# Where the operands of 17,280 matmuls stand in SBUF: high and low parts side by side, moving operands 0 or 256 bytes (modulo 512) from the weights loaded beside them

## The chip, the cores and the metric

The kernel runs on one core of one Trainium2 chip. The metric is the device time of one execution in microseconds, the median of several runs. All weights come from HBM in every execution; nothing of them stays on the chip between executions.

## What is computed

One inference step of a two-layer trunk with model width 2048 for a prompt of 256 new tokens and 8 samples of 4 tokens each, which share the weights. Layer 0 mixes by retention and a gated linear recurrence, layer 1 by a diagonal state-space model (S5) and a GLU; both end in a SwiGLU feed-forward (FFN) with 5632 hidden channels.

```python
# per layer (rmsnorm, silu and gelu as usual)
out, *states = even_mixer(x, ...)   # layer 0: w_in 2048x6144, retention | conv + RG-LRU, w_out 2048x2048
out, *states = odd_mixer(x, ...)    # layer 1: S5 scan, gelu, w_glu 2048x4096, z1 * sigmoid(z2)
x = x + out
x = x + swiglu(rmsnorm(x, g))       # w_gu 2048x11264, w_dn 5632x2048
y = rmsnorm(x, g_final)
# returned: y of the prompt and of the samples, and the new states
```

256 + 32 tokens make 288 columns, N in the code.

## The kernel before

**The products.** Channels lie on partitions and tokens along the free dimension, so every dense product is a row of matmuls of one shape: a stationary 128 x 128 block of weights, a moving operand of 128 x 288. float32 inputs go through the fast float32r path by splitting each operand into a high part (what float32r keeps) and a low part (the rest), and by summing three products in PSUM for each block k of the contraction, in this order (lines 315 to 317 in `run_prog`):

```python
pe.matmul(acc, lhsT=wh[:, o:o + P], rhs=xh, start=(k == u.k0), stop=False)
pe.matmul(acc, lhsT=wh[:, o:o + P], rhs=xl, start=False, stop=False)
pe.matmul(acc, lhsT=wl[:, o:o + P], rhs=xh, start=False, stop=(k == u.k1 - 1))
```

I call these three a triple. While one matmul streams its moving operand, TensorE loads the weights of the next one from SBUF. So the high part of a chunk streams beside the load of the same block of `wh` (for the second matmul), the low part beside the load of a block of `wl`, and the high part once more beside the load of the next block of `wh`.

**The weights.** `run_prog` walks through all units (one unit is 128 output channels) in slots of up to 8 blocks. For each slot SP loads `raw` by DMA (ring of 4), ScalarE writes the high part `wh` (ring of 4, line 268), VectorE the low part `wl` (line 274, which appears as line 99; 3 buffers, from the first FFN on a fourth, `wlx`). All of them are tiles of 128 x 1024 float32, 4096 bytes in each partition. A block is 512 bytes long, so within one ring all blocks start at the same place modulo 512. In the built program that is byte 32 for `raw`, `wh` and the three `wl`, and byte 288 for `wlx`.

**The moving operands.** A chunk is 128 x 288 float32, 1152 bytes in each partition, which is 2 x 512 + 128. Chunks come out of pools (helpers `xg_`, `xl_`, `ac_`, called through `split`), which hand out a ring of buffers that lie one after the other:
- `xg_`, `xl_`: 16 high parts and behind them 16 low parts of the normed input (w_in, FFN 0, and the high parts of FFN 1). From one chunk to the next both move by 128 bytes modulo 512.
- `ac_`: one ring in which high and low parts alternate (20 buffers in the first phase, 30 later), for the input of w_out, the hidden channels of both FFNs and the high parts of the GLU's input. High and low part of one chunk are 128 bytes apart modulo 512, and the next chunk of a unit stands wherever the ring had come to.
- `x2`: the low parts of FFN 1's input, in a pool that is opened after the S5 stage (line 1583).

With weights at byte 32 (or 288) a moving operand stands at 0, 128, 256 or 384 bytes from the weights loaded beside it, and in the program before these four are taken by 4504, 4095, 4250 and 4113 of the matmuls that another of these follows (some 240 have other distances, in w_out).

**Other buffers.** `g_` hands out scratch tiles of a ring: 11 in the first phase, 14 later (`phase_open`). The order of the instructions is that of the Python code: `later` puts a step some slots further on, and each engine runs its queue in order.

**The S5 stage** (`s5_core`) has small matmuls of 72 columns between which VectorE works. Matmuls without use, `warm` (line 1475), keep TensorE going there: 24 ahead of the stage and 8, 8, 8 and 16 in its first four steps, all with weights at column 512 of a `wh` tile and a moving operand from column 0 on, so 0 bytes apart modulo 512; they have 64 or 128 columns of weights and 128, 288 or 512 moving columns.

## Time and profile before

| | |
|---|---|
| median of 3 runs | 2492.91 us (2488.81 to 2494.98) |
| the profiled execution | 2491.51 us, of which the span is 2489.7 us |
| TensorE busy | 2449.2 us, 98% of the span |
| VectorE, ScalarE, GpSimd busy | 66%, 46%, 6% |
| DMA | 198 GB/s on average |
| granted TensorE clock, mean | 0.996 |

The program runs w_in and w_out to about 460 us, FFN 0 to about 1340 us, S5 with the first part of the GLU to about 1480 us, the rest of the GLU to about 1630 us, and FFN 1 to the end. A matmul's duration in a row (about 295 ns) is its latency from first read to last write; matmuls overlap, so what counts is the distance from one start to the next, which is read from timelines, or from the number of matmuls in a window.

### The profile page before, as it was taken

To read this page: it belongs to the slowest core of one execution; us is meant where nothing else is said; L and a number is where in the kernel's file an instruction comes from. 1 tells how busy PE (TensorE), PEld (TensorE's weight loads), DVE (VectorE), ACT (ScalarE), POOL (GpSimd) and SP (SyncE) were. 2 spreads that over 40 slices of the span, in tenths; PEclk is the share of its full clock that TensorE was granted. 3 is DMA by queue.
4 is the path that set the end of the run, shared out by engine and by line. 5 is a ranking of instruction groups with operands and counts; after the bars stand their busy time and mean duration, and the time that the engine had idled before them with its cause. 6 is when DMAs were issued, how large, how long until landed. Compare 5 with 4: busy or idle time off the path is not lost.

```text
span 2489.7 us, 49585 instructions
## 1 busy us (share of the span) xinstructions
PE 2449.2 (98%) x20130; PEld 2419.2 (97%) x20130; DVE 1638.0 (66%) x3033; ACT 1145.3 (46%) x1756; POOL 154.2 (6%) x299
## 2 busy tenths in 40 slices
PE   8999999999999999999999999999999999999997
PEld 8999999999999999999998899999999999999997
DVE  7767676567677878778856996655544555445554
ACT  6656554533355445555543554443333333333343
POOL 0111110000010121111110000000000000000000
PEclk9999999999999999999999999999999999999999
DMA  7655655555577777777797875555555555555553
GB/s 250 192 183 187 214 163 172 168 163 165 185 243 250 254 257 249 257 262 227 241 294 223 291 235 159 184 164 162 165 163 171 162 167 157 169 167 163 162 164 127
DMA packets 168612, 493.78 MB, mean 198 GB/s; under 512 B 30400, under 2 KB 42944, under 8 KB 168128
## 3 DMA queue, kind: packets, MB, share of 16 engines
q1 hardware_dynamic: 152192, 439.51, 55.7%
q0 software_dynamic: 15184, 49.77, 5.7%
q8 instruction: 159, 2.61, 0.4%
q10 hardware_dynamic: 1008, 1.33, 0.1%
q14 instruction: 69, 0.57, 0.1%
HBM read 449.16 MB, written 48.19 MB: 200 GB/s over the span
## 4 chain that ended last, share of the span: by engine, by line
PE 92%; DVE 4%; DMA 2%; ACT 1%; issue 1%; SPq 0%; DVEq 0%; ACTq 0%
PE acc L315 30%; PE acc L317 29%; PE acc L316 29%; DVE w L99 1%; DVE wl L99 1%; DMA tab<-tabO 1%; DMA raw<-in_w_glu_dram 1%; DMA raw<-in_w_in_dram 1%; DMA tab<-tabR 0%; DVE w L1459 0%; PE mp L775 0%; PE mp L520 0%; PE mp L1310 0%; ACT wh L268 0%; PE mp L723 0%
## 5 line engine op out<-in xcount | busy, mean ns | idle before, releaser
L315 PE MATMUL acc<-xg,wh 128*128 128x288 f32 x3520 | 1045.6, 297 | 0.0
L268 ACT ACTIVATE wh<-raw 128x1024 fp32r<-128x1024 f32 (+2 forms) x758 | 760.4, 1010 | 427.6 <-PE acc L316 262.7
L317 PE MATMUL acc<-xg,wl 128*128 128x288 f32 x2816 | 828.1, 294 | 1.3 <-DVE wl L99 1.3
L316 PE MATMUL acc<-xl,wh 128*128 128x288 f32 x2624 | 773.8, 295 | 0.0
L99 DVE TENSOR_TENSOR wl<-raw,wh 128x1024 fp32r<-128x1024 f32 (+3 forms) x601 | 697.5, 1173 | 24.6 <-ACT wh L268 16.3
L315 PEld LDWEIGHTS acc<-xg,wh 128*128 128x128 f32 x3520 | 659.6, 187 | 1.8 <-issue 0.8
L315 PE MATMUL acc<-ac,wh 128*128 128x288 f32 x2080 | 616.7, 297 | 2.0 <-ACT ac L1594 1.1
L317 PEld LDWEIGHTS acc<-xg,wl 128*128 128x128 f32 x2816 | 530.4, 188 | 1.5 <-DVE wl L99 1.5
L316 PEld LDWEIGHTS acc<-xl,wh 128*128 128x128 f32 x2624 | 493.0, 188 | 0.5
L317 PE MATMUL acc<-ac,wl 128*128 128x288 f32 x1626 | 480.8, 296 | 3.4 <-DVE wl L99 2.4
L316 PE MATMUL acc<-ac,wh 128*128 128x288 f32 x1568 | 462.6, 295 | 0.0
L316 PE MATMUL acc<-x,wh 128*128 128x288 f32 x1408 | 415.4, 295 | 0.0
L315 PEld LDWEIGHTS acc<-ac,wh 128*128 128x128 f32 x2080 | 391.6, 188 | 4.8 <-ACT ac L1594 1.3
L99 DVE TENSOR_TENSOR g<-acc,rstd 128x288 f32<-128x288 f32 x192 | 87.7, 457 | 347.5 <-PE acc L317 346.9
L317 PEld LDWEIGHTS acc<-ac,wl 128*128 128x128 f32 x1626 | 306.5, 189 | 5.9 <-DVE wl L99 5.9
L316 PEld LDWEIGHTS acc<-ac,wh 128*128 128x128 f32 x1568 | 296.1, 189 | 0.0
L316 PEld LDWEIGHTS acc<-x,wh 128*128 128x128 f32 x1408 | 264.3, 188 | 0.1
L317 PE MATMUL acc<-xg,wlx 128*128 128x288 f32 x704 | 207.0, 294 | 0.0
L99 DVE TENSOR_TENSOR X<-X,acc 128x288 f32<-128x288 f32 x112 | 50.9, 455 | 233.7 <-PE acc L317 233.4
L99 DVE TENSOR_TENSOR wlx<-raw,wh 128x1024 fp32r<-128x1024 f32 (+3 forms) x157 | 178.6, 1138 | 17.9 <-ACT wh L268 17.7
L194 ACT ACTIVATE ac<-g 128x288 fp32r<-128x288 f32 x98 | 43.5, 444 | 283.8 <-DVE g L99 283.8
L317 PE MATMUL acc<-ac,wlx 128*128 128x288 f32 x454 | 133.7, 295 | 0.1
(294 smaller groups left out, 2038.2 us busy)
## 6 DMA issues: line engine op xcount, KB each, us to landing
raw<-in_w_gu_dram SPq DMA_DIRECT2D x352, 512.0 KB, 4.6
raw<-in_w_dn_dram SPq DMA_DIRECT2D x128, 448.0 KB, 4.2
raw<-in_w_in_dram SPq DMA_DIRECT2D x96, 512.0 KB, 4.7
raw<-in_w_dn_dram SPq DMA_DIRECT2D x64, 512.0 KB, 3.7
raw<-in_w_out_dram SPq DMA_DIRECT2D x32, 512.0 KB, 4.3
raw<-in_w_glu_dram SPq DMA_DIRECT2D x40, 384.0 KB, 4.2
raw<-in_w_glu_dram SPq DMA_DIRECT2D x32, 320.0 KB, 4.0
out_ret_s_dram<-s POOLq DMA_DIRECT2D x16, 512.0 KB, 5.2
```

Of the source, the lines that this page charges most:

```text
L99: v.tensor_tensor(o, a, b, op=op)
L194: act.activation(h, x, AF.Copy, scale=scale)
L268: act.activation(wh[:, :w], raws[i][:, :w], AF.Copy)
L315: pe.matmul(acc, lhsT=wh[:, o:o + P], rhs=xh, start=(k == u.k0), stop=False)
L316: pe.matmul(acc, lhsT=wh[:, o:o + P], rhs=xl, start=False, stop=False)
L317: pe.matmul(acc, lhsT=wl[:, o:o + P], rhs=xh, start=False, stop=(k == u.k1 - 1))
```

## The change

No product, no weight and no order of work is changed, apart from the `warm` matmuls. What changes is where tiles lie:
- `xgp` and the `act` pool have one buffer for each name instead of a ring, and `next_` takes the names in turn. Since a name's place is given at its first use, and `split` now takes the low part before the high part, the tiles of a pair lie side by side: low, high, low, high. A pair is 2304 bytes, which is 4 x 512 + 256, so from pair to pair every high part moves by 256 bytes modulo 512, and so does every low part.
- `ac_` gets a sister, `al_`, for low parts: 10 + 10 names instead of 20 buffers, later 15 + 15 instead of 30.
- a pad of 128 bytes, `wpad`, stands between `raw` and `wh` (byte 32) and the `wl` tiles, which so come to byte 160, `wlx` included. In the built program all high parts in these pools are at byte 32 or 288 and all low parts at 160 or 416.
- the input of FFN 1 is cut from two large tiles at a step of 1536 bytes, high parts in one, low parts in the other.
- the scratch ring has 10 buffers instead of 11, later 13 instead of 14.
- the `warm` matmuls all get 128 columns of weights and 288 moving columns: 32 ahead of the S5 stage, of which 8 are 0, 8 are 256, 8 are 128 and 8 again 256 bytes apart, and 8 in each of the first four steps, at 0, 128, 256 and 384 bytes. (Weights from column 512 on, moving operand from column b on.)

In the built program 10,450 of the 17,280 matmuls are then 256 bytes from the weights loaded beside them and 6432 are 0 bytes from them; some 320 have other distances, in w_out.

```diff
-    xgp = ctx.enter_context(tc.tile_pool(name="xgp", bufs=16))
+    xgp = ctx.enter_context(tc.tile_pool(name="xgp", bufs=1))
...
+    def next_(k, n):
+        turn[k] = turn.get(k, -1) + 1
+        return turn[k] % n
+
     def xg_(dt=F32R):
-        return xgp.tile([P, N], dt, tag="x", name=nm("xg"))
+        return xgp.tile([P, N], dt, tag=f"x{next_('x', 16)}", name=nm("xg"))
...
-    def ac_(dt=F32R, w=N):
-        return AP_["p"].tile([P, AP_["w"]], dt, tag="a", name=nm("ac"))[:, :w]
+    def ac_(dt=F32R):
+        return AP_["p"].tile([P, N], dt, tag=f"a{next_('a', AP_['n'])}", name=nm("ac"))
+
+    def al_(dt=F32R):
+        return AP_["p"].tile([P, N], dt, tag=f"al{next_('al', AP_['n'])}", name=nm("al"))
...
     def split(x, scale, alloc, alloc_l=None, lag=True):
+        l = (alloc_l or alloc)()
         h = alloc()
         act.activation(h, x, AF.Copy, scale=scale)
-        l = (alloc_l or alloc)()
...
+        for tag in ("raw", "wh"):
+            wt.tile([P, 1024], F32R if tag == "wh" else F32, tag=tag, name=nm(tag))
+        wt.tile([P, 32], F32, name="wpad", bufs=1)
         ring = [wt.tile([P, 1024], F32R, name=f"wl{k}", bufs=1) for k in range(3)]
...
-    ph = phase_open(11, 20, N, 6)
+    ph = phase_open(10, 10, 6)
...
-        return split(x, 0.5, ac_)
+        return split(x, 0.5, ac_, al_)
...
-                    hid[t] = split(u, 0.5, ac_)
+                    hid[t] = split(u, 0.5, ac_, al_)
...
-        phase_open(14, 30, N, 0)
+        phase_open(13, 15, 0)
...
-        def warm(ps, n, m, w=N):
+        def warm(ps, n, b):
             xw = S["whs"][min(S["whs"])]
             for k in range(n):
-                o = 32 * (k % 4) if m == 32 else 0
-                pe.matmul(ps[o:o + m, :w], lhsT=xw[:, 512:512 + m], rhs=xw[:, :w], start=True, stop=True,
-                          tile_position=(0, o), skip_group_check=True)
+                pe.matmul(ps[k % len(ps)][:, :N], lhsT=xw[:, 512:640], rhs=xw[:, b:b + N], start=True, stop=True,
+                          skip_group_check=True)
...
-                warm(po, *((8, P), (8, 64), (8, 64), (16, P, P))[j])
+                warm([po], 8, 32 * j)
...
-            h, l = ac_(), xl_()
+            h, l = (ac_ if j < NT - 1 else al_)(), xl_()
...
-        pw = ps5.tile([P, 512], F32, tag="o", name=nm("po"))
-        warm(pw, 10, P, 512)
-        warm(pw, 8, 64)
-        warm(pw, 2, P, 512)
-        warm(pw, 4, P, 512)
+        pw = ps5.tile([P, 2, 512], F32, tag="p", name=nm("pp"))
+        for b in (0, 64, 32):
+            warm([pw[:, 0]], 8, b)
+        warm([pw[:, 0], pw[:, 1]], 8, 64)
...
-        S["x2"] = S["st2"].enter_context(tc.tile_pool(name="x2", bufs=16))
+        S["x2"] = S["st2"].enter_context(tc.tile_pool(name="x2", bufs=1))
...
-        fin = final_hook(V_FFN1, {}, "xg", lambda: S["x2"].tile([P, N], F32R, tag="x", name=nm("x2")))
+        def x2(k):
+            if ("y", k) not in turn:
+                turn["y", k] = S["x2"].tile([P, 384 * NT + 96], F32R, tag=f"y{k}", name=f"x2{k}")
+            i = 384 * next_(k, NT) + 64
+            return turn["y", k][:, i:i + N]
+        fin = final_hook(V_FFN1, {}, "xg", lambda: x2(0), lambda: x2(1))
```

On every engine the instructions stand in the same order before and after, under other tile names, with one exception on TensorE ahead of and in the S5 stage. There the queue of TensorE reads before (`po` and `pp` are PSUM tiles, `tab` a table of the S5 stage, `xg` its input, `Hs` its states; lines 1435, 1489 and 1499 are the small matmuls):

```order
L1416 MATMUL po_16591<-nacc_15595,ones 32x72 x4
L1479 MATMUL po_16611<-wh_16469 128x512 x10
L1479 MATMUL po_16611<-wh_16469 64x288 x8
L1479 MATMUL po_16611<-wh_16469 128x512 x6
L1435 MATMUL pp_16637<-xg_15683,tab_15850 64x72 x16
L1435 MATMUL pp_16657<-xg_15746,tab_15856 64x72 x16
L1479 MATMUL po_16683<-wh_16469 128x288 x8
L1489 MATMUL po_16683<-xg_15683,tab_15854 32x72 x16
```

And in the changed kernel, at the same place:

```order
L1429 MATMUL po_16594<-nacc_15598,ones 32x72 x4
L1491 MATMUL pp_16614<-wh_16472 128x288 x32
L1448 MATMUL pp_16648<-xg_15686,tab_15853 64x72 x16
L1448 MATMUL pp_16668<-xg_15749,tab_15859 64x72 x16
L1491 MATMUL po_16694<-wh_16472 128x288 x8
L1501 MATMUL po_16694<-xg_15686,tab_15857 32x72 x16
```

The 24 `warm` matmuls of two shapes have become 32 of one shape, in the PSUM tile that the stage's first real matmuls use next; nothing else has moved.

Waits on released buffers differ in a few places, since pools are laid out otherwise. The one that changes engine is on ScalarE in the GLU, at the first high part of FFN 1's input. Before (`wh` from `raw` are weights, `xg` is the high part, `nacc` the sum of squares; DMASW are GpSimd's DMA queues, through which the S5 states leave):

```order
L268 ACTIVATE wh2807_19043<-raw2799_18972 128x768 [waits DMAHW2_49,PE_49,Activation_49]
L268 ACTIVATE wh2810_19064<-raw2802_18994 128x640 [waits DMAHW3_49,PE_49,Activation_49]
L194 ACTIVATE xg2814_19087<-X_76,vec_74 128x288 [waits DVE_49]
L173 ACTIVATE nacc2813_19086<-X_76 128x288
L268 ACTIVATE wh2816_19091<-raw2805_19018 128x640 [waits DMAHW4_49,PE_49,Activation_49]
```

And after:

```order
L281 ACTIVATE wh2809_19046<-raw2801_18975 128x768 [waits DMAHW2_49,PE_49,Activation_49]
L281 ACTIVATE wh2812_19067<-raw2804_18997 128x640 [waits DMAHW3_49,PE_49,Activation_49]
L205 ACTIVATE x20_19091<-X_76,vec_74 128x288 [waits DMASW3_49,DMASW4_49,DVE_49,Pool_49]
L183 ACTIVATE nacc2815_19089<-X_76 128x288
L281 ACTIVATE wh2816_19094<-raw2807_19021 128x640 [waits DMAHW4_49,PE_49,Activation_49]
```

The wait for the end of the S5 tables' space, which VectorE had ahead of the first low part, is ScalarE's now, ahead of the first high part.

## Rows read from the trace of the kernel before

**Rows 1.** The page, part 1: busy time, share of the span, instructions of each engine.
```profile
PE 2449.2 (98%) x20130; PEld 2419.2 (97%) x20130; DVE 1638.0 (66%) x3033; ACT 1145.3 (46%) x1756; POOL 154.2 (6%) x299
```

**Rows 2.** Waits of TensorE: line, who was waited for, us in total, times, longest.
```profile
PE mp L315 <- ACT xg L355: 7.4, 1, 7.4
PE po L1499 <- ACT ac L1522: 4.2, 3, 2.5
PE acc L317 <- DVE wl L99: 3.7, 5, 1.3
```

**Rows 3.** Groups of line 315 on TensorE: count, busy us, mean ns, idle before.
```profile
L315 PE MATMUL acc<-xg,wh 128*128 128x288 f32 x3520 | 1045.6, 297 | 0.0
L315 PE MATMUL acc<-ac,wh 128*128 128x288 f32 x2080 | 616.7, 297 | 2.0 <-ACT ac L1594 1.1 <-ACT wh L268 1.0
L315 PE MATMUL acc<-l,wh 128*128 128x288 f32 x96 | 28.3, 295 | 0.0
L315 PE MATMUL mp<-xg,wh 128*128 128x288 f32 x64 | 21.0, 327 | 7.4 <-ACT xg L355 7.4
```

**Rows 4.** Windows of TensorE: us, busy us (matmuls), granted clock, DMA share, GB/s.
```profile
1700.00:1800.00 100.00, 100.00 (x753) 1.00 0.53 168
1800.00:2400.00 600.00, 600.00 (x4506) 1.00 0.51 164
```

**Rows 5.** Timeline of TensorE in FFN 1: start us, duration us, instruction.
```profile
1700.78 0.29 PE L315 MATMUL acc<-xg,wh 128*128 128x288 f32 x1
...
1701.18 0.30 PE L315 MATMUL acc<-xg,wh 128*128 128x288 f32 x1
...
1701.58 0.29 PE L315 MATMUL acc<-xg,wh 128*128 128x288 f32 x1
```

**Rows 6.** Timeline of TensorE in the GLU, first and last of eleven starts.
```profile
1489.56 0.29 PE L316 MATMUL acc<-xl,wh 128*128 128x288 f32 x1
...
1490.86 0.29 PE L317 MATMUL acc<-ac,wlx 128*128 128x288 f32 x1
```

**Rows 7.** Timeline of TensorE in the GLU, six starts in a row.
```profile
1492.81 0.29 PE L317 MATMUL acc<-ac,wl 128*128 128x288 f32 x1
1492.94 0.29 PE L315 MATMUL acc<-ac,wh 128*128 128x288 f32 x1
1493.07 0.30 PE L316 MATMUL acc<-xl,wh 128*128 128x288 f32 x1
1493.21 0.29 PE L317 MATMUL acc<-ac,wl 128*128 128x288 f32 x1
1493.34 0.29 PE L315 MATMUL acc<-ac,wh 128*128 128x288 f32 x1
1493.47 0.29 PE L316 MATMUL acc<-xl,wh 128*128 128x288 f32 x1
```

**Rows 8.** Timeline of TensorE in FFN 1's second product, first and last of 25 starts.
```profile
2136.58 0.29 PE L315 MATMUL acc<-ac,wh 128*128 128x288 f32 x1
...
2139.82 0.29 PE L315 MATMUL acc<-ac,wh 128*128 128x288 f32 x1
```

**Rows 9.** Warm matmuls of S5's steps 0 and 2: timeline, then durations min/median/max ns.
```profile
1354.12 1.32 PE L1479 MATMUL po<-wh 128*128 128x288 f32 x8
1367.88 1.26 PE L1479 MATMUL po<-wh 128*64 128x288 f32 x8
L1479 PE MATMUL po<-wh x8: 290/294/401, 1354.1 to 1355.1; 128*128 128x288 f32 x8
L1479 PE MATMUL po<-wh x8: 288/293/346, 1367.9 to 1368.8; 128*64 128x288 f32 x8
```

**Rows 10.** Warm matmuls of S5's step 1: timeline of TensorE.
```profile
1363.07 2.08 PE L1479 MATMUL po<-wh 128*64 128x288 f32 x8
```

**Rows 11.** The chain of waits ahead of S5: start us, us, what.
```profile
1347.12 4.91 PE po L1479 x24
1353.24 1.30 DVE w L99 x2
```

**Rows 12.** Window at the start of S5: us, busy of PE, PEld, DVE, ACT, POOL, clock.
```profile
1356.00:1364.00 8.00, 5.20 (x107) 4.78 (x101) 7.61 (x13) 2.00 (x6) 0.36 (x1) 0.63 0.65 225
```

**Rows 13.** FFN 1's low parts on VectorE: durations, first and last start.
```profile
L108 DVE SCALAR_TENSOR_TENSOR x<-X,vec,xg x16: 510/514/516, 1494.2 to 1634.5; 128x288 fp32r<-128x288 f32 x16
```

More of the change, by code (lines that the diff above doesn't have):

```diff
@@ L69, in gp_ @@
         return AP_["gen"].tile([P, TOK], dt, tag="g", name=nm("g"))[:, :w]
+    turn = {}
+    def next_(k, n):
+        turn[k] = turn.get(k, -1) + 1
+        return turn[k] % n
     def xg_(dt=F32R):
-        return xgp.tile([P, N], dt, tag="x", name=nm("xg"))
+        return xgp.tile([P, N], dt, tag=f"x{next_('x', 16)}", name=nm("xg"))
     def xl_():
-        return xgp.tile([P, N], F32R, tag="xl", name=nm("xl"))
-    def ac_(dt=F32R, w=N):
-        return AP_["p"].tile([P, AP_["w"]], dt, tag="a", name=nm("ac"))[:, :w]
+        return xgp.tile([P, N], F32R, tag=f"xl{next_('xl', 16)}", name=nm("xl"))
+    def ac_(dt=F32R):
+        return AP_["p"].tile([P, N], dt, tag=f"a{next_('a', AP_['n'])}", name=nm("ac"))
+    def al_(dt=F32R):
+        return AP_["p"].tile([P, N], dt, tag=f"al{next_('al', AP_['n'])}", name=nm("al"))
     AP_ = {}
@@ L83, in mp_, with phase_open @@
         return AP_["ps"].tile([P, 512], F32, tag="m", name=nm("mp"))
-    def phase_open(gb, ab, aw, pb):
+    def phase_open(gb, ab, pb):
         st = AP_["st"] = ExitStack()
         AP_["gen"] = st.enter_context(tc.tile_pool(name=nm("gen"), bufs=gb))
-        AP_["p"] = st.enter_context(tc.tile_pool(name=nm("act"), bufs=ab))
-        AP_["w"] = aw
+        AP_["p"] = st.enter_context(tc.tile_pool(name=nm("act"), bufs=1))
+        AP_["n"] = ab
+        turn["a"] = turn["al"] = -1
         if pb:
@@ L851, in yl_evac, with final_hook @@
         return evac
-    def final_hook(gcol, accbox, lstname, alloc_l=xl_):
+    def final_hook(gcol, accbox, lstname, alloc=xg_, alloc_l=xl_):
         def fin(j):
@@ L859, in fin @@
             if gcol is not None:
-                xs[lstname].append(split(x, vec[:, gcol + j:gcol + j + 1], xg_, alloc_l))
+                xs[lstname].append(split(x, vec[:, gcol + j:gcol + j + 1], alloc, alloc_l))
             norm_acc(accbox["acc"], j, x)
@@ L1596, in first @@
             return Unit(w, 0, k1, lambda: xs["y"], ev)
-        g1 = [first(("g", j), ins["w_glu"][NT + j], 4 if j < 12 else 6, lambda: ac_(F32)) for j in range(NT - 2)]
+        g1 = [first(("g", j), ins["w_glu"][NT + j], 4 if j < 12 else 6, lambda: al_(F32)) for j in range(NT - 2)]
         g1 += [first(("z", j), ins["w_glu"][j], 6, lambda: xg_(F32)) for j in range(NT - 2)]
```

## The prediction, made before the changed kernel ran

> **What bounds the kernel now.** I read the busy times first. TensorE is busy for 2449.2 of 2489.7 us, VectorE for 66% [rows 1]. That alone could be a row of long matmuls with waits hidden in them, so I read the waits of TensorE next: the longest total is 7.4 us, once, at the start, and the next are about 4 us [rows 2]. TensorE practically never waits for another engine. So the time is the number of its matmuls times the distance between their starts.
>
> The number: line 315 has 3520 + 2080 + 96 + 64 = 5760 matmuls [rows 3], and lines 316 and 317 follow it one for one, so there are 17,280 of 128 x 288. The distance: in the window from 1800 to 2400 us there are 4506 matmuls, of which two or three reach in from before it, so 600 / 4503 = 133.2 ns; from 1700 to 1800 us it is the same [rows 4]. 17,280 x 133.2 ns = 2302 us of the 2489.7. A nanosecond in this distance is worth 17.3 us. Nothing else in the program is worth looking at beside it, as long as the change adds no wait.
>
> **What the distance depends on, before.** 288 columns at 2.4 GHz, which is the granted clock of 1.00 in these windows, are 120 ns. So some 13 ns come on top of the streaming. Does the place of the operands have a part in that? The trace of before holds a natural experiment, since all four distances modulo 512 occur in it. I put the built program's addresses beside the starts. Four patterns are of use; by *good* I mean 0 or 256 bytes, by *bad* 128 or 384.
> - In FFN 1's first product, whole triples are good and bad in turn. A triple takes 0.40 us whichever it is: from 1700.78 to 1701.18 to 1701.58 [rows 5], so 133.3 ns per matmul.
> - In one stretch of the GLU good and bad change with each single matmul. Eleven starts lie within 1489.56 to 1490.86 us, so ten distances of 130.0 ns [rows 6].
> - A little later come five good ones in a row, an accident of the ring: from 1492.81 to 1493.47 us, 132 ns each [rows 7].
> - In FFN 1's second product, where high and low part differ and good ones often meet from one triple to the next, 24 distances lie within 2136.58 to 2139.82 us: 134.9 ns [rows 8].
>
> So one and the same form of matmul, at the same clock and with no wait, goes at 130.0 to 134.9 ns depending on the pattern. Place has an effect. But it isn't a simple sum over good and bad pairs, for rows 5 and rows 6 have the same half of good ones and differ by 3.3 ns.
>
> The Trainium skill speaks against any such effect: in TensorE: Matmul & The Clock Gate, section "Step-by-step: what each phase is for", it says that TensorE has two independent SBUF read ports and that loading the next tile's weights doesn't steal read bandwidth from the running matmul. By that rule the change would be worth nothing at all. Rows 6 against rows 8 don't agree with it.
>
> **The change part by part.**
>
> *All operands good.* After the change nearly all 17,280 are good, in one long row. The trace has such rows only where they are short. In place, with real weights, rows 7 give 132 ns (five distances, read to 0.01 us, so by 2 ns uncertain). The warm matmuls are the second witness, since all of them are 0 bytes apart: the eight of step 0 have 128 columns of weights and 288 moving columns like the real ones, and take 1.32 us from the first start to the last end. Take off the last one's latency of 0.294 us and the first one's late start of 0.401 - 0.294 = 0.107 us, and seven distances are left in 0.919 us: 131.3 ns. With 64 columns of weights, in step 2, it is (1.26 - 0.293 - 0.053) / 7 = 130.6 ns [rows 9]. The warm matmuls load one block again and again; the real ones change it and share rows 7's neighbours, so I take rows 7's 132.0 ns, and keep 131.3 and 132.6 (the middle between 132 and the 133.2 of rows 4) as its bounds. Before, the mean is a little under 133.2, since the GLU has faster stretches; I take 133.1 (an estimate from rows 4 and 6). So the saving is 1.1 ns x 17,280 = 19 us, with bounds of 0.5 ns (9 us) and 1.8 ns (31 us). It lies wholly on the path, since TensorE is the path. No row has 256 bytes alone; that it equals 0 is taken from the patterns above, in which I find no difference between the two.
>
> *Is another engine next?* A slot of 8 blocks is 24 matmuls, 3.2 us; after the change 3.17 us. VectorE is at 66% over the span [rows 1], so 1% more speed on TensorE uncovers nothing.
>
> *Side by side instead of a ring.* The tiles are handed out in the same turn, so each buffer is free at the same moment as before. In the first phase ten of each kind replace 20 mixed ones, one pair per chunk in both. Cost nothing; what hides it is that the buffer was read a whole third of the FFN ago.
>
> *A scratch buffer less.* Ten instead of 11, 13 instead of 14: a scratch tile is asked for again one allocation earlier. The steps that would wait are on ScalarE (46% busy) and VectorE, ahead of weights that are prepared three slots, some 9.6 us, before TensorE needs them. TensorE's three largest waits for ScalarE and VectorE, at the start, in S5 and for `wl`, add to 15.3 us over the whole program [rows 2], so I take 0; if the cover fails, some single wait of the size of rows 2's small ones, 1 to 4 us.
>
> *The wait moved to ScalarE in the GLU.* VectorE's first low part started at 1494.2 us [rows 13] behind the same wait for the S5 space. ScalarE's high part comes just ahead of it, and behind it are the sums of squares and `wh` for later slots. If the DMAs were late by a microsecond, three prepared slots hide it. Cost 0.
>
> *The warm matmuls.* Ahead of S5 they are on the chain of waits: 24 take 4.91 us, and VectorE follows at 1353.24 [rows 11]. 32 of the new form take 32 x 0.131 + 0.1 = 4.3 us: 0.6 us less. In the four steps they stand beside VectorE, which is busy for 7.61 of 8 us there [rows 12], so they cost nothing as long as they are done before it is. Those of step 1 took 2.08 us for eight [rows 10], and the granted clock of that window is 0.63 of full speed [rows 12], so part of it ran at 1.2 and part at 2.4 GHz. If all four groups ran at that rate it would be 8.3 us instead of 6.7, at worst 1.7 us more. I take -0.5 us together, with -2 and +2 as ends.
>
> *Sum,* made against the profiled execution: 2491.5 - 19 - 0.5 = 2472.0 us. That execution is 1.4 us under the median of the runs, so I leave it at that: 2472.
>
> **The rivals.**
>
> *A: the forecast,* 132 ns: 2472 us, from 2460 (131.3 ns) to 2483 (132.6 ns).
>
> *B: nothing happens.* The 133.3 ns of rows 5 is what TensorE falls into whenever the pattern is steady, whatever the place; only an irregular pattern leaves it. For it: rows 5 hold good triples and bad ones at exactly the same 0.40 us, and a good triple isn't faster by a hair there. Against it: rows 9 are steady too, and are at 131.3. Then the change costs 0.2 ns x 17,280 = 3.5 us: 2495 us, and 2485 to 2499 around it. The rule of the Trainium skill cited above (TensorE: Matmul & The Clock Gate, section "Step-by-step: what each phase is for") would leave the time at that of before too.
>
> *C: good pairs are much better than rows 7 say.* In rows 6 half the pairs are bad. If those take the 133.3 ns of rows 5, the good ones take 126.7, for the mean is 130.0. A whole program of these saves 6.4 ns x 17,280 = 111 us: 2381. For it: rows 6 is the cleanest stretch. Against it: rows 7 and rows 9, which have nothing but good ones and stay above 130.
>
> *D: slower.* What pays is the change between good and bad from one matmul to the next, and good ones behind each other get into each other's way. Rows 8 have many such meetings, and go at 134.9. If the changed program goes at that rate throughout, it loses 1.8 ns x 17,280 = 31 us: 2523. It decides from 133.5 ns on. For it: rows 6 against rows 8. Against it: rows 7.
>
> **How the numbers follow.** A 0.50, B 0.29, C 0.09, D 0.12. The predicted time is A's. A measurement of this kernel can tell about 0.3%, 7.5 us, from no change, so A's upper end just reaches "same". Faster: 0.48 of A and C's 0.09, 0.57. Same: the rest of A and most of B, 0.29. Slower: D and the end of B, 0.14. The range has to leave out 0.2: it leaves out C and D, and goes from 2445 us (130.4 ns, A's mechanism at the 64-column rate of rows 9 with the reading error) to 2500 (B with the S5 costs against it).
>
> **What would show it.** In windows of FFN 1 the number of matmuls per 100 us: 753 before, 758 to 762 for A, 753 for B, about 790 for C, under 747 for D. A triple in the timeline: 0.396 us for A, and the same at each place. The warm groups of the changed kernel are eight each at 0, 256 and 128 bytes: if A is right, those at 0 and 256 take the same time. The waits of TensorE should still have nothing over 8 us in total; a new row there, for ScalarE's `g` or for `x2`, would show a scratch buffer or the moved wait uncovered. I am wrong if the distance doesn't become the same in all stages, or if the time falls without the distance falling.

## The result, and the profile after

The changed kernel takes **2470.89 us** (median of 4 runs, 2469.42 to 2474.32) against 2491.44 us before (4 runs on the same chip): a ratio of 0.9917, 95% interval 0.9904 to 0.9929, so 20.5 us less. The forecast was 2472, with a range of 2445 to 2500. The profiled execution took 2469.42 us, with a span of 2467.7.

First the busy time of TensorE, from the page of the changed kernel (part 1), beside [rows 1]:

```profile
PE 2426.4 (98%) x20130; PEld 2397.4 (97%) x20130; DVE 1636.6 (66%) x3033; ACT 1144.8 (46%) x1756; POOL 154.6 (6%) x299
```

As many matmuls as before, 22.8 us less of busy time, and no other engine has changed. The waits of TensorE (line, who was waited for, us in total, times, longest), beside [rows 2]:

```profile
PE mp L328 <- ACT xg L368: 6.9, 1, 6.9
PE po L1511 <- ACT ac L1534: 4.8, 3, 2.5
PE acc L330 <- DVE wl L109: 3.0, 6, 1.3
```

The same three waits, of the same size. No new row for a scratch buffer, for the `x2` tiles or for the wait that went to ScalarE. So the gain is the distance between matmuls, as in [rows 4]. Windows of TensorE after the change (from:to us, length, busy us and matmuls, granted clock, share of the DMA engines, GB/s):

```profile
820.00:860.00 40.00, 40.00 (x303) 1.00 0.71 229
1700.00:1800.00 100.00, 100.00 (x765) 1.00 0.52 168
1800.00:2400.00 600.00, 600.00 (x4578) 1.00 0.52 167
```

4578 in 600 us where there were 4506: 600 / 4575 = 131.1 ns in FFN 1, less than the 132 of the forecast. But in the 40 us of the first window it is 40 / 300.5 = 133.1 ns, the pace of before. So the pace isn't the same everywhere. The timeline shows both cleanly (start us, duration us, instruction). Every third matmul in FFN 1:

```profile
1700.06 0.29 PE L328 MATMUL acc<-x,wh 128*128 128x288 f32 x1
...
1700.45 0.29 PE L328 MATMUL acc<-x,wh 128*128 128x288 f32 x1
...
1700.85 0.29 PE L328 MATMUL acc<-x,wh 128*128 128x288 f32 x1
...
1701.24 0.29 PE L328 MATMUL acc<-x,wh 128*128 128x288 f32 x1
```

And every third in FFN 0, while the tables are being made:

```profile
839.72 0.30 PE L328 MATMUL acc<-xg,wh 128*128 128x288 f32 x1
...
840.12 0.30 PE L328 MATMUL acc<-xg,wh 128*128 128x288 f32 x1
...
840.52 0.30 PE L328 MATMUL acc<-xg,wh 128*128 128x288 f32 x1
...
840.92 0.30 PE L328 MATMUL acc<-xg,wh 128*128 128x288 f32 x1
```

1.18 us for three triples is 131.1 ns a matmul; 1.20 us is 133.3. In both, all operands lie at 0 or 256 bytes. Where does the one become the other? Around the first table chunk:

```profile
724.00 0.29 PE L330 MATMUL acc<-ac,wl 128*128 128x288 f32 x1
...
724.39 0.29 PE L330 MATMUL acc<-ac,wl 128*128 128x288 f32 x1
...
724.78 0.29 PE L330 MATMUL acc<-ac,wl 128*128 128x288 f32 x1
725.01 1.08 PE L1323 MATMUL mp<-vzt,pst 128*32 128x128 f32 x32
...
726.39 0.30 PE L330 MATMUL acc<-ac,wl 128*128 128x288 f32 x1
...
726.79 0.30 PE L330 MATMUL acc<-ac,wl 128*128 128x288 f32 x1
...
727.19 0.30 PE L330 MATMUL acc<-ac,wl 128*128 128x288 f32 x1
```

0.39 us a triple up to the 16 small matmuls of line 1323 (the profile records 32), 0.40 us right after them, with the same tiles. It stays so over all eight chunks, up to some 1290 us, where TensorE waits 1.2 us for a `wh` and 1.3 us for a `wl`. Means of all distances from 0.11 to 0.2 us, from every start in the traces, by stretch of the program:

```
trace, us          before          after           e10 (below)
w_in                133.2           131.6           131.6
w_out               132.8           131.9           131.9
FFN 0, no tables    133.1           131.1           131.1
FFN 0, tables       133.0           133.3           131.1
S5, GLU             132.3           131.6           131.6
FFN 1               133.2           131.1           131.1
all                 133.0           131.8           131.3
```

(Some 4,100 matmuls are in the fourth line, 6,300 in the last stretch.) 1.2 ns x 17,280 = 21 us is the whole gain.

In w_in, too, a few stretches are slow. Three rows of 143 matmuls there begin right behind the same small matmuls of line 636, each time after the same wait of 0.56 us. In windows of 18 us, one in each row:

```profile
120.00:138.00 18.00, 18.00 (x137) 1.00 0.54 183
212.00:230.00 18.00, 18.00 (x140) 1.00 0.48 141
302.00:320.00 18.00, 18.00 (x137) 1.00 0.47 145
```

From their starts the three rows go at 133.3, 131.1 and 133.3 ns, each at one pace to its end, and in e10 below the same three rows go at the same three paces.

### The profile page after: what moved, and what is told of

Same layout as the page of the kernel before. It is cut to its first block, busy times and chain, and to the rows that moved or that the text cites. A ratio compares the mean times of both kernels' runs of the same rounds, so it can differ in the third digit from the quotient of the medians.

```text
span 2467.7 us, 49587 instructions
## 1 busy us (share of the span) xinstructions
PE 2426.4 (98%) x20130; PEld 2397.4 (97%) x20130; DVE 1636.6 (66%) x3033; ACT 1144.8 (46%) x1756; POOL 154.6 (6%) x299
## 4 chain that ended last, share of the span: by engine, by line
PE 95%; DVE 2%; DMA 2%; issue 0%; ACT 0%; SPq 0%; DVEq 0%; ACTq 0%
PE acc L329 30%; PE acc L330 30%; PE acc L328 30%; DVE w L109 1%; PE po L1511 1%; DMA raw<-in_w_in_dram 1%; DVE wl L109 1%; PE pp L1448 0%; PE mp L788 0%; DMA raw<-in_w_dn_dram 0%; PE mp L533 0%; PE mp L1323 0%; PE mp L736 0%; DMA tab<-tabR 0%; PE mp L710 0%
## 5 line engine op out<-in xcount | busy, mean ns | idle before, releaser
L328 PE MATMUL acc<-xg,wh 128*128 128x288 f32 x2112 | 625.5, 296 | 0.0
L328 PE MATMUL acc<-ac,wh 128*128 128x288 f32 x2048 | 603.9, 295 | 2.2 <-ACT wh L281 1.2
L330 PE MATMUL acc<-xg,wl 128*128 128x288 f32 x1760 | 519.8, 295 | 0.0
L329 PE MATMUL acc<-al,wh 128*128 128x288 f32 x1568 | 465.9, 297 | 0.0
L329 PE MATMUL acc<-x,wh 128*128 128x288 f32 x1408 | 418.2, 297 | 0.0
L328 PE MATMUL acc<-x,wh 128*128 128x288 f32 x1408 | 412.1, 293 | 0.0
L328 PEld LDWEIGHTS acc<-xg,wh 128*128 128x128 f32 x2112 | 398.1, 188 | 1.7 <-issue 0.8
L328 PEld LDWEIGHTS acc<-ac,wh 128*128 128x128 f32 x2048 | 386.1, 189 | 4.7 <-ACT wh L281 1.4
L330 PE MATMUL acc<-x,wl 128*128 128x288 f32 x1056 | 309.9, 293 | 0.0
L329 PEld LDWEIGHTS acc<-al,wh 128*128 128x128 f32 x1568 | 295.3, 188 | 0.0
L328 PEld LDWEIGHTS acc<-x,wh 128*128 128x128 f32 x1408 | 264.7, 188 | 0.1
L329 PEld LDWEIGHTS acc<-x,wh 128*128 128x128 f32 x1408 | 264.0, 188 | 0.1
```

## The experiments

Three questions: is it the place at all, or only that now all matmuls of a chunk are alike (theory D, the distance, against theory R, the regularity)? Why do the same places go at 131.1 and at 133.3 ns (theory S: the same addresses have two steady paces, and each interruption of the stream chooses one)? And is there a better place than 0?

### All bad, in the same regularity (e2)

```diff
+        wt.tile([P, 32], F32, name="wpad0", bufs=1)
         for tag in ("raw", "wh"):
...
+        wt.tile([P, 32], F32, name="wpad1", bufs=1)
```

(and the same around `wlx`). All triples are now at 128 or 384 bytes.

> The changed kernel with pads of 128 bytes so that every moving operand lies 128 or 384 bytes (mod 512) from the weights loaded beside it, in place of 0 or 256: the same regularity, the other distance. Theory D (distance): the pace is 133.2 ns or more, about 2494 us or slower, and no stretch at 131.1 ns. Theory R (regularity alone, all three matmuls of a chunk alike): the same as the changed kernel, 131.8 ns, 2471 us. Theory S (two states whatever the place): also about 2471 us, with 131.1 and 133.3 ns in other stretches.

Measured: 2493.41 us (10 runs), ratio to before 1.0011 (1.0002 to 1.0020). The window of FFN 1:

```profile
1700.00:1800.00 100.00, 100.00 (x753) 1.00 0.53 166
1800.00:2400.00 600.00, 600.00 (x4503) 1.00 0.52 164
```

133.3 ns. One shift by 128 bytes, nothing else, takes the whole gain away: 22.5 us between two kernels of the same regularity. R is refuted; the place of the moving operand beside the weights counts. (That the weights alone stand elsewhere is not the reason: in e13 below all tiles move together by 128 bytes, and the pace is 131.1 ns in the old place and in the new one.)

### Only the low part bad (e3)

```diff
-        wt.tile([P, 32], F32, name="wpad", bufs=1)
```

> The changed kernel without the 128-byte pad ahead of the ring of low weight parts: the low moving part is at 128 or 384 bytes of its neighbour weights while the two others are at 0 or 256, so within nearly every chunk the places change (good bad good, 2,971 chunks, or bad good bad, 2,149). Theory D (distance, mean of what stands beside): between the changed kernel and the kernel before, 132.2 ns, about 2478 us. Theory R (any change of place costs): 133.2 ns or slower, 2495 us. From the alternating stretch of the kernel before (130.0 ns, rows 6) one would even expect less than the changed kernel: 131 ns, 2457 us, where the chunks happen to alternate from one to the next.

Measured: 2477.14 us (4 runs), ratio 0.9942 (0.9925 to 0.9959); in FFN 1:

```profile
1800.00:2400.00 600.00, 600.00 (x4540) 1.00 0.52 166
```

132.2 ns, just what D says, and between the other two. The hope from [rows 6] did not come true. That D fits so well is partly luck: in this trace the pace goes from 131.1 ns in some stretches of FFN 0 to 133.3 in parts of the GLU, and the combinations in e6 below don't follow such a mean.

### Good and bad in turn (e5)

```diff
+    ring_(xgp, F32R, ("x", 16), ("pad", 1), ("xl", 16))
...
+        ring_(AP_["p"], F32R, *((("pre", 0), ("a", ab)) + ((("pad", 1),) if ab % 2 == 0 else ()) + (("al", ab),)))
...
-            i = 384 * next_(k, NT) + 64
+            i = N * next_(k, NT)
```

(`ring_` hands out all tiles of a ring ahead, one behind the other; `wpad` is gone.)

> The same tiles as in the changed kernel, but placed so that good (0 or 256 bytes) and bad (128 or 384 bytes) alternate from each matmul to the next: all high parts of a ring one behind the other, then all low parts, 128 bytes further on modulo 256. Half of all pairs are bad. Theory D (distance): worse than the changed kernel, 132.5 to 133.2 ns, 2483 to 2495 us. Theory R (regularity): no better than 131.8 ns, 2471 us. What rows 6 showed in the kernel before (a strictly alternating stretch at 130.0 ns) says 130.0 to 130.3 ns for 16,800 of 17,280 matmuls: 2440 to 2447 us, faster than both kernels.

Measured: 2489.38 us (10 runs), ratio 0.9990 (0.9981 to 0.9999): no gain worth the name, where [rows 6] had promised 45 us. The trace has both paces, for one and the same alternation. The timeline of TensorE in `w_in`, first and last of eleven starts:

```profile
145.30 0.29 PE L336 MATMUL acc<-xg,wl 128*128 128x288 f32 x1
...
146.60 0.29 PE L334 MATMUL acc<-xg,wh 128*128 128x288 f32 x1
```

And in FFN 1, first and last of ten starts:

```profile
1699.96 0.29 PE L334 MATMUL acc<-x,wh 128*128 128x288 f32 x1
...
1701.16 0.29 PE L334 MATMUL acc<-x,wh 128*128 128x288 f32 x1
```

1.30 us for ten distances and 1.20 for nine: 130.0 and 133.3 ns. Within `w_in` alone the same alternation goes at 133.3 ns in other stretches (from 200 to 220 us, for one). So the alternation of [rows 6] was not by itself what made that stretch quick; it can go at either pace. What chose the pace there, no run shows.

### The old warm matmuls in the changed kernel (e4)

```diff
-        def warm(ps, n, b):
+        def warm(ps, n, m, w=N):
...
-                warm([po], 8, 32 * j)
+                warm(po, *((8, P), (8, 64), (8, 64), (16, P, P))[j])
```

> The changed kernel with the warm matmuls of the kernel before (8 x 288, 8 and 8 of 64 weight columns, 16 of 128 columns, and 10 + 8 + 2 + 4 ahead of the recurrence, up to 512 columns) in place of the new ones; all places as in the changed kernel. If the new places alone make the gain: 2471 us plus the term put on the warm matmuls, 0.5 us (2469 to 2473), so 20 us faster than the kernel before. If the warm matmuls carry a part of the gain through the clock that they set up: up to 2480 us.

Measured: 2470.57 us (4 runs), against 2470.89: no difference. On the chain of waits (start us, us, what) the group ahead of S5 in the changed kernel, beside [rows 11]:

```profile
1339.12 4.43 PE pp L1491 x32
```

The same in this kernel, with the old ones:

```profile
1338.16 4.92 PE po L1492 x24
```

The new ones save 0.49 us there, as the term said; in the whole it can't be told from nothing. So the `warm` matmuls carry no measurable part of the gain, and e2 showed that the places carry it.

### A bench of 32 distances (e1)

In `finish`, ahead of the last norm, matmuls of the kernel's form on tiles of their own; the weights stay, the moving operand moves on by 16 bytes from group to group:

```diff
+        def sweep(b):
+            for k in range(32):
+                w = wcol()
+                pe.matmul(m1[:, :N], lhsT=mw[0][:, w:w + P], rhs=mw[1][:, b:b + N], start=True, stop=True, skip_group_check=True)
```

> The changed kernel with a bench of about 4,300 more matmuls (128 x 288, weights 128 x 128) ahead of its last norm, in which TensorE alone works (no DMA, no other engine); the block makes the program some 600 us longer, and only the distances inside it are read. It holds 32 distances between moving operand and weights (steps of 16 bytes over 512), seven patterns of good (0, 256) and bad (128, 384) distances, each after seven kinds of small interruption, and one good pattern after 24 interruptions of 1 to 24 small matmuls. Theory D (the distance sets the pace): 0 and 256 bytes at 131 ns, 128 and 384 at 133 to 135 ns, whatever came before them. Theory R (only regularity counts): every distance alike, 131 to 132 ns. Theory S (two steady paces of the same addresses, chosen at each interruption and kept to the next): the good pattern comes out at 131.1 ns after some of the 24 interruptions and at 133.3 ns after others. If the slow pace of the stretch at 736 to 1300 us came from DMA traffic or other engines instead, none of the 24 is at 133.3 ns, since nothing else runs here.

Groups of 32 in the timeline at 0, 16, 32, 112, 128, 256 and 272 bytes:

```profile
2465.84 4.48 PE L1685 MATMUL mp<-wh,wh 128*128 128x288 f32 x32
2470.51 4.42 PE L1685 MATMUL mp<-wh,wh 128*128 128x288 f32 x32
2475.13 4.53 PE L1685 MATMUL mp<-wh,wh 128*128 128x288 f32 x32
...
2498.47 4.57 PE L1685 MATMUL mp<-wh,wh 128*128 128x288 f32 x32
2503.24 4.53 PE L1685 MATMUL mp<-wh,wh 128*128 128x288 f32 x32
...
2540.83 4.48 PE L1685 MATMUL mp<-wh,wh 128*128 128x288 f32 x32
2545.50 4.43 PE L1685 MATMUL mp<-wh,wh 128*128 128x288 f32 x32
```

The last 24 distances of each group (from the starts) come to 131.7, 130.0, 133.3, 134.9, 133.3, 131.7 and 130.0 ns; 48 bytes too is at 130.0. The distance counts with no other engine at work, 256 bytes is a period, and 0 isn't the best place. Theory S missed: after all 24 interruptions the good pattern went at 131.7 ns. Two other patterns of this bench bear on what follows. A strict alternation of 0 and 128 bytes went at 133.3 ns after all seven kinds of interruption, never at 130.0. And one good matmul with two bad ones went at 132.2 ns after five kinds and at 131.1 after the two with 16 small matmuls: the first sign of S.

### The kernel's own triples (e6)

The second bench has two weight tiles and two moving tiles, in triples.

> The changed kernel with a second bench of about 10,900 more matmuls ahead of its last norm, TensorE alone, some 1,450 us longer; only the distances inside it are read. The matmuls come in the kernel's own triples (high weights with high part, high weights with low part, low weights with high part), the places alternating between 0 and 256 bytes from chunk to chunk, accumulating in one bank. First, 60 matmuls at distance 0 and 60 at distance 16 bytes after each of 20 interruptions (1 to 16 small matmuls of 128 columns, and 16 of 64, 72, 96 and 120); then all 16 x 16 combinations of the distances of the high and the low part in steps of 16 bytes. Theory S (two paces of the same addresses, chosen at the interruption): at distance 0 some of the 20 groups are at 131.1 ns and some at 133.3 ns. If that slow pace of the stretch at 736 to 1300 us came from other engines or DMA traffic, all 20 are at 131.1 ns. Theory D (distance, period 256 bytes, as in the first bench): equal distances of 16 and 48 bytes at 130.0 ns, 0, 64 and 96 at 131 to 132, 32, 128 and 160 to 224 at 133.3, 112 at 134.9; unequal ones near the mean of the two, high part counting twice.

At distance 0 all 20 groups went at 131.7 ns: S missed again. At 16 bytes, though, 4 of the 20 went at 130.0 and 16 at 131.7. The first two of them, after 1 and after 2 small matmuls:

```profile
2645.30 8.06 PE L1673 MATMUL mp<-wh,wh 128*128 128x288 f32 x60
2653.64 8.17 PE L1673 MATMUL mp<-wh,wh 128*128 128x288 f32 x60
```

So S exists, but not for this layout at 0. What the bench lacked: in the kernel the low pair, weights and moving part, lies 128 bytes behind the high pair. In the 16 x 16 table unequal distances did not follow the mean of the two either (144 and 224 bytes gave 128.9 ns, after the single interruption tried there).

### 16 bytes, in the kernel (e7)

```diff
-            wh = wt.tile([P, 1024], F32R, tag="wh", name=nm("wh"), bufs=LH + 1)
+            o = 1024 * (i % (LH + 1)) + 4
+            wh = whr[:, o:o + 1024]
```

(likewise the tiles of `wl` and `wlx`, with pads.)

> The changed kernel with its weight tiles shifted so that every moving operand lies 16 or 272 bytes (mod 512) from the weights loaded beside it, in place of 0 or 256; the four tiles of high weights and the three of low weights become slices of one tile each, nothing else changes. Theory D (the distance sets the pace, by the first bench 130.0 ns at 16 bytes): 130.0 to 130.5 ns against 131.8, 17,280 x 1.3 to 1.8 = 22 to 31 us less than the changed kernel, 2440 to 2449 us. Theory R (only regularity counts): 2471 us, the same as the changed kernel. If operands off the 64-byte grid slow the other engines that write them, TensorE waits for weights or moving parts, and the time is above 2471 us.

Measured: 2485.33 us (10 runs), ratio 0.9978 (0.9969 to 0.9988), so 14 us slower than the changed kernel where 22 to 31 less were expected. FFN 1:

```profile
1800.00:2400.00 600.00, 600.00 (x4527) 1.00 0.52 165
```

132.6 ns. TensorE waits for nothing new. The distance that is best in the bench isn't in the kernel, so the distance alone is not the whole rule. This kernel has a second pace as well, in the stretch of the tables, and it changes in the middle of it:

```profile
820.00:860.00 40.00, 40.00 (x304) 1.00 0.78 258
1110.00:1150.00 40.00, 40.00 (x302) 1.00 0.79 268
```

From the starts the pace is 132.6 ns after the first two table chunks and 133.3 after the other six, up to S5, though all eight have the same 16 small matmuls.

### The layout of the kernel in the bench (e8)

Now with the low pair 128 bytes further on.

> The changed kernel with a third bench of about 16,000 more matmuls ahead of its last norm, TensorE alone, some 2,200 us longer; only the distances inside it are read. Triples as in the second bench, but now also with the low weights and the low part both 128 bytes further on, as the rings lie in the changed kernel: first 20 interruptions, with 60 matmuls after each, for distance 0 laid out so (all chunks alike; then chunks alternating between 0 and 256 bytes); then the same for distances of 16, 48 and 144 bytes with the low pair 0 and 128 bytes further, for two unequal pairs of the second bench (144 and 224, 144 and 192), and a table of six distances by 16 offsets of the low pair, each after two interruptions. Theory S (two paces of the same addresses, chosen at the interruption): laid out as in the changed kernel, distance 0 gives 131.1 ns after some interruptions and 133.3 after others. Theory D (the distance alone sets the pace): 131.7 ns in all, as in the second bench, whatever the offset of the low pair; the slow stretch at 736 to 1300 us then has another cause (other engines, DMA). A third case, P (the offset between the two pairs counts as well as the distance): 131.1 ns in all 20 with the offset of 128 bytes, against 131.7 without, and other values along the 16 offsets. For 16 bytes: 132.6 ns with the offset of 128 (as measured in the kernel e7), 130.0 or 131.7 without.

This answers the second question in part: the same addresses do have two paces. Distance 0, laid out as in the changed kernel, after 13 small matmuls and after 14, with no DMA and no other engine:

```profile
2579.17 8.12 PE L1673 MATMUL mp<-wh,wh 128*128 128x288 f32 x60
...
2588.22 8.27 PE L1673 MATMUL mp<-wh,wh 128*128 128x288 f32 x60
```

131.1 and 133.3 ns over the last 48. Of the 20 groups the 13 after 1 to 13 small matmuls are at 131.1, the 7 after 14 to 16 (four of them after 16 narrower ones) at 133.3; with chunks that change between 0 and 256 it is the same, but for 4 small matmuls, which left 133.3. The number by itself is no rule: in the last bench (e13) the same layout was at 131.1 after 16. Case P holds as well: 16 bytes with the offset of 128 gave 132.5 to 132.7 ns after all 20 interruptions, without it 130.0 or 131.7; e7 was at 132.6, but for its slower stretch at 133.3, which the bench did not show. The pair of 144 and 224 bytes has three paces here: 128.9 ns after 3 of the 20 interruptions, 131.1 after 4 and 133.3 after 13. So one quick group, as in the second bench, says little.

### The table chunks split (e10)

If the 16 small matmuls of a chunk leave the slow pace behind and 8 would leave the quick one, the stretch must get quicker when they are issued 8 at a time.

```diff
+        def tt_():
+            tt_half(0)
+            later(1, tt_tail)
```

(`tt_half` has one `jj` of the old loop; `tt_tail` does the other half and what followed.)

> The changed kernel with one edit in the table chunks: the 16 small matmuls of a chunk (32 weight columns, 128 columns) are issued 8 at a time, with one half unit of the main stream between, in place of 16 in one row. Nothing else moves, and the work is the same. Theory S (the interruption chooses the pace; in the third bench 8 small matmuls left 131.1 ns behind and 14 to 16 left 133.3): the 4,060 matmuls at 736 to 1300 us run at 131.1 in place of 133.3 ns, 4,060 x 2.2 = 9 us, less 8 more interruptions at some 0.3 us each, 2 to 3 us: 2464 us (2461 to 2466). If the slow pace there comes from other engines or DMA: 133.3 ns as before and 2473 us.

Measured: **2464.2 us** (4 runs, 2463.67 to 2466.48), ratio to before 0.9890 (0.9873 to 0.9906): faster than both kernels, and 6.7 us less than the changed one. Windows in the stretch of the tables:

```profile
820.00:860.00 40.00, 40.00 (x307) 1.00 0.76 247
970.00:1010.00 40.00, 40.00 (x307) 1.00 0.77 242
```

307 where there were 303, at more DMA traffic, not less (247 against 229 GB/s). All eight stretches between chunks are at 131.1 ns. The 9 us of pace less the eight more interruptions give what was expected. So the pace of this stretch hangs on how the stream is interrupted, in the kernel as in the bench, and not on DMA or other engines. Whether it is the number of small matmuls in a row or the moment at which they come, this run doesn't tell: both changed. And the kind of interruption isn't the whole rule, as the three rows of w_in and the table chunks of e7 show.

### A better layout: found in the bench, lost in the kernel (e9, e11, e13)

The fourth bench goes through the 256 places that the weights can take when the two moving parts lie as they do.

> The changed kernel with a fourth bench of about 19,700 more matmuls ahead of its last norm, TensorE alone, some 2,700 us longer; only the distances inside it are read. It looks for a place that the kernel's rings can take without more room: low part 128 bytes behind the high part (modulo 256, as two tiles of 1,152 bytes side by side give), all 16 places of the high weights and all 16 of the low weights in steps of 16 bytes, each after 8 and after 16 small matmuls of 128 columns; then two layouts (112 bytes with both weights alike, and 144 bytes with the low weights 128 bytes on) after 1 to 16 small matmuls. By the third bench the layout of 144 bytes is at 131.1 ns after all 16. Theory S: most layouts have one or two steady paces, all between 128.9 and 135 ns, the layout of the changed kernel 131.1 after 8 and 133.3 after 16. If the distance alone counted, the layouts would fall into rows and columns, each the mean of the paces at its distances (high counting twice).

The layout of the changed kernel gave 131.1 after 8 and 133.3 after 16. The paces lay between 128.9 and 135.6 ns and did not fall into rows and columns. The best, after 8 and after 16, has the high part 144 bytes from the high weights and the low weights 48 bytes behind those:

```profile
4049.72 4.57 PE L1673 MATMUL mp<-wh,wh 128*128 128x288 f32 x33
...
4055.23 4.52 PE L1673 MATMUL mp<-wh,wh 128*128 128x288 f32 x33
```

128.9 ns over the last 18. In the kernel, with pads and slices as in e7:

> The changed kernel with its weight tiles shifted by other pads: the moving high part 144 bytes (modulo 256) from the high weights, the low weights 48 bytes on from the high ones, the low part 128 bytes behind the high part as it was; the four tiles of high weights become slices of one tile. In the fourth bench this layout was at 128.9 ns after both interruptions, the lowest of 256. If the bench carries over (the pace is set by the whole layout of the four tiles): 128.9 ns against 131.8, 17,000 x 2.9 = 49 us less than the changed kernel, 2421 us, with single stretches slower where an interruption chooses another pace; if half of the stretches do so (131.1 to 133.3), 2440 to 2460 us. Theory D (the distance alone): the distances here are 144 (twice) and 224 bytes, by the first bench 131.1, 131.1 and 133.3, mean 131.8 ns, 2471 us, as the changed kernel. If operands off the 64-byte grid slow the engines that write them, TensorE waits for weights, which the kernel e7 (16 bytes) did not show.

Measured: 2484.72 us (9 runs), ratio 0.9974 (0.9964 to 0.9984). 132.8 ns in all long stretches, and never 128.9:

```profile
1800.00:2400.00 600.00, 600.00 (x4521) 1.00 0.52 164
```

All places relative to each other were those of the bench. What differed: in the bench the weights began on a multiple of 32 bytes and the moving parts 16 behind one; in the kernel it was the other way round. The last bench shifts all four tiles together.

> The changed kernel with a fifth bench of about 8,600 more matmuls ahead of its last norm, TensorE alone, some 1,160 us longer; only the distances inside it are read. Two layouts, that of the kernel e11 (128.9 ns in the fourth bench, 132.8 ns in the kernel) and that of the changed kernel, each with all four tiles shifted together by 0 to 240 bytes in steps of 16, after 2, 4, 8 and 16 small matmuls, 48 matmuls each; and 450 matmuls in one row for shifts of 0 and 112 bytes, the latter the place of the tiles in e11. If only the places of the four tiles relative to each other count: each layout has the same pace at all 16 shifts, 128.9 ns and 131.1 (or 133.3). If the place on the absolute grid counts too: 128.9 ns at shift 0 and 132.8 at 112. If the row of 33 matmuls in the fourth bench was too short to be steady: 128.9 ns in the first matmuls of the long rows and 132.8 in their last 48.

Four windows in rows of 450: shift 0 twice, shift 112 (as in e11) twice:

```profile
2920.00:2970.00 50.00, 50.00 (x390) 1.00 0.00 1
2980.00:3030.00 50.00, 50.00 (x390) 1.00 0.00 1
3040.00:3090.00 50.00, 50.00 (x378) 1.00 0.00 1
3100.00:3150.00 50.00, 50.00 (x378) 1.00 0.00 1
```

128.9 and 132.8 ns, steady to the end. At the eight shifts that are multiples of 32 bytes it is 128.9 to 129.1 after all four interruptions, at the eight others 132.8. The layout of the changed kernel is at 131.1 (133.3 in two of 32) on the multiples of 32 and at 131.8 to 131.9 off them. So the absolute place counts too. (The weights of e7 also began 16 bytes off a multiple of 32.) A kernel with the weights on such a multiple and the moving parts 16 bytes off it was not run; from these rows 17,280 x 2.3 ns, some 40 us less than e10, is an estimate, for the case that no interruption in the kernel picks another pace.

## Why the prediction was right, step by step

- **What bounds it: right.** TensorE waited no more and no less than before; 21 us come out of the distances.
- **The distance depends on the place: right**, and shown by e2: 22.5 us for a shift of 128 bytes. The rule that the prediction weighed, that loading weights doesn't take read bandwidth from the running matmul (the Trainium skill, TensorE: Matmul & The Clock Gate, section "Step-by-step: what each phase is for"), would leave the place without effect; that doesn't agree with e2, nor with the 128.9 to 135.6 ns of one form of matmul in the benches, where TensorE is alone. Whether it is bandwidth that is taken, no run shows.
- **132.0 ns from [rows 7]: right as a mean, wrong as a pace.** The mean is 131.8. The rows themselves were read 0.4 ns too high: from the full starts in the trace the five distances are 131.6 ns, which would have made 2465. But no long stretch ran at one pace of 132.0: three quarters of the matmuls are in stretches with means of 131.1 to 131.9, a quarter, in the table stretch, at 133.3. FFN 1 had 765 per 100 us where A said 758 to 762, and the triple took 0.393 or 0.400 us, not 0.396. The prediction's own condition, that the distance become the same in all stages, was not met: the table stretch did not gain at all (133.0 before, 133.3 after). What failed is the step from a pattern of places to one pace. Places give a few steady paces, and the pace can change at an interruption (e8, e10). That the mean came out so near is partly luck: with the table chunks issued otherwise the same change gives 2464.
- **Rival B: right for that quarter.** "133.3 is what TensorE falls into" holds there, though not for the reason given: with the same places and another interruption that quarter goes at 131.1 (e10). In e2, with all operands bad, the means of the table's stretches are 132.8 to 133.3.
- **0 and 256 alike: right** (131.7 and 131.7 in the first bench). The warm rows at 131.3, which the prediction set aside for [rows 7], were the better witness for a long row.
- **C and D: refuted.** Both took [rows 6] and [rows 8] as properties of a pattern. e5 has the pattern of [rows 6] nearly everywhere and is at 133.1 ns in the mean. The distances there are long and short in turn, from the starts 134.8 and 131.7 ns in FFN 1, and 132.0 and 128.0 in the quick stretch at 145 us; neither is the 133.3 and 126.7 of C. And nothing but good operands gives 131.1 to 133.3 in the changed kernel, neither C's 126.7 nor D's 134.9.
- **The warm matmuls, -0.5 us: right** (4.91 to 4.43 us on the chain, which is the forecast size; in the whole e4 shows no difference, so there it is not shown).
- **Side by side, a scratch buffer less, the wait on ScalarE, each 0: right**; no new row among the waits. They were not taken apart in runs of their own.

## What to carry to other kernels

Where TensorE is the whole path, count the matmuls in windows of equal length over the program: a stretch with 1 or 2% fewer at the same clock and without waits is worth a look at where the operands lie and at what interrupted the stream last. A pace seen in a short stretch is no property of its pattern until it has been seen after other interruptions too. And a bench must copy the kernel's layout in full (relative and absolute places, all four tiles), else its best place is not the kernel's.

## What the runs showed of the hardware

- One form of matmul (128 x 288, 128 columns of weights, granted clock 1.00, no waits) has mean distances from 128.9 to 135.6 ns in the fourth bench, by the places in SBUF of moving operand and weights.
- In the first bench the pattern repeats with 256 bytes (distances 0 and 256: 131.7; 16 and 272: 130.0; 128 and 384: 133.3). Places 16 bytes apart differ; finer steps were not tried. With all tiles moved together, multiples of 32 bytes differ from the places between them (128.9 against 132.8).
- Some layouts have two paces or more (131.1 and 133.3; 130.0 and 131.7; 128.9, 131.1 and 133.3). Which one it is can change at an interruption, and it lasted to the next: in FFN 1 for 6,300 matmuls, in the table stretch over eight chunks, each of which left the slow one.
- Why the places act so, and by what rule an interruption leaves one pace or the other, no run here shows. The same interruption left different paces in w_in (133.3, 131.1, 133.3).
